# A feed-forward convolution whose third tap moves from VectorE to ScalarE and an adding DMA transfer

## The chip, the cores and the metric

The kernel runs on one core of a Trainium2 chip. The metric is the device time of one execution in microseconds (us). A profile of one execution gives the start and duration of each instruction on TensorE (PE, with its weight loads as PEld), VectorE (DVE), ScalarE (ACT), GpSimd (POOL) and the DMA queues that SyncE (SP) and GpSimd issue.

## What is computed

One layer of a hybrid decoder: a mixer (stick-breaking attention beside a gated convolution), then a feed-forward block with a causal convolution of three taps between its up-projection and its activation. The change lies in the feed-forward block. Its reference, for 1024 positions and 1024 channels, with 2 x 2816 columns of `w_up`:

```python
def causal_dwconv(u, w):              # y[t] = w[0] u[t-2] + w[1] u[t-1] + w[2] u[t]
    up = jnp.pad(u, ((0, 0), (kw - 1, 0), (0, 0)))
    y = up[:, 0:s, :] * w[0]
    for i in range(1, kw):
        y = y + up[:, i:i + s, :] * w[i]
    return y

h = rms_norm(x, norm_ffn_pre[l])
u = causal_dwconv(h @ w_up[l], conv_ffn_w[l])
a, g = jnp.split(u, 2, axis=-1)
f = (jax.nn.gelu(g, approximate=True) * a) @ w_down[l]
x = x + rms_norm(f, norm_ffn_post[l])
```

## The kernel before

Channels lie on the 128 partitions and positions along the free dimension, so the 2816 columns of a and of g are 22 tiles f of 128 channels, each a buffer of 128x1024 float32. Products are made with float16 pairs (a high half and a low half of each operand), three matmuls for one product, in block schemes that save one block product in eight: each tile f has seven products, `up_prod(f, 1..7)`, of twelve matmuls each. Their sums leave PSUM by ScalarE copies and VectorE additions into two buffers `ca` and `cg`. The bank `b` of a tile takes the products 1, 6, 7 and 4 in turn, so the eviction of one must be over before the next starts.

`up_done(f)` then runs `conv` for `ca` into `ua` and for `cg` into `ug`: ScalarE writes `u = w2 * c` (line 1527), VectorE adds the taps with lags 1 and 2 (line 1529, two instructions). ScalarE applies gelu to `ug` in place (line 1539), VectorE multiplies it into `ua` (line 1540), and ScalarE sums the squares (line 66) for the scale of the float16 halves.

The tiles are in six groups of 4, 4, 4, 4, 3 and 3. The sums of squares of a group are added over partitions by a one-column matmul `pr_f` on TensorE from VectorE's `rb_f`; its result `sp_f` scales the halves `fa`, `fy`, `fs` and `fx` (high half by ScalarE on line 824, low half by VectorE on line 826). For each of the first four groups a stage follows of seven products with `w_down`, each in four tiles of positions (`pq`, line 1656). ScalarE evicts `pq` to `st` (line 1660), and GpSimd's queue adds each `st` of 512 KB to a partial sum `acc` in memory (line 790; the first group writes plainly). One more pair of up-products, that of product 4 and `up_done` of the tile f in hand, stands inside each stage behind its first product. Weights are loaded by SyncE (`ws_u`, `ds`), their squares summed by ScalarE (`jk_u`), reduced through `rb_u` and `pr_u` like the above, and converted into `wh_u` and `wq`. `join` reads the partial sums back (`u`, `yacc`), and the last two groups are multiplied plainly into `pd` (lines 1726 and 1759), whose VectorE evictions add to `yacc`; the closing norm and the output follow.

The order on every engine is written by a planner, `Plan`: each step has an engine, a cost, the buffers that it reads and writes, and perhaps a due time; TensorE's main products keep the order of the program (`seq`), and the rest is placed by readiness and lateness, in a model that counts buffers, too. Large buffers (`ca`, `cg`, `ua`, `ug`, `st`, `ds`, the halves) share 16 slots of one pool, `slab`; a slot is taken again when its last reader is done. An engine runs its instructions in the order written, and so does each DMA queue issue.

Of the kernel before, what the change touches and what calls it, by code (L numbers as in the profile page):

```python
# [20 lines left out]
AF = mybir.ActivationFunctionType  # L21
ALU = mybir.AluOpType
# [3 lines left out]
T = 1024  # L26
# [4 lines left out]
NFF = FF // P  # L31
# [16 lines left out]
class Layer:  # L48
# [692 lines left out]
    def rest(self):  # L741
# [14 lines left out]
        C = dict(Asq=0.82, A=0.97, Ah=0.5, As=1.04, Ash=0.6, Aq=1.18, V=1.21, Vh=0.64, Vp=0.72)  # L756
        vec, act, pe = nc.vector, nc.scalar, nc.tensor

        DUE = {"conv": 20.0, "fin": 25.0, "ev": 3.0, "pass": 5.0, "hn": 14.0}
# [19 lines left out]
        def V(cost, fn, r, w, **kw):  # L779
            return pl.add("V", cost, fn, r, w, **kw)  # L780

        def A(cost, fn, r, w, **kw):
            return pl.add("A", cost, fn, r, w, **kw)
# [4 lines left out]
        def load(eng, b, dst, srcf, mb=1.45, r=(), w=None, ahead=None, **kw):  # L788
            e = nc.sync if eng == "SP" else nc.gpsimd
            j = pl.add(eng, 0.45 if eng == "SP" else 1.14, lambda: e.dma_start(dst(), srcf(), **kw), r,  # L790
                       [b] if w is None else w, ahead=AHEAD["load"] if ahead is None else ahead)
            j.load, j.lag = mb, pl.LAG[eng]
            return j
# [40 lines left out]
        AHEAD = dict(load=45.0, sq=40.0, up=32.0, quad=40.0, wq=60.0, wp=40.0, join=20.0, pr=3.0, cv=1.0, ca=1.0, mb=2.7)  # L834
        AHEAD.update(self.ahead_set)
        C = {k: v * AHEAD["ca" if k[0] == "A" else "cv"] for k, v in C.items()}
# [631 lines left out]
        def up_prod(f, i):  # L1468
# [16 lines left out]
            def vadd(o, oc, og, x, xr):  # L1485
                V(C["Vp"], lambda: vec.tensor_tensor(o.t[:, oc], b.t, x.t[:, xr[0]], ALU.add),
                  [b, (x, xr[1])], [(o, og)])
# [17 lines left out]
            else:  # L1505
# [13 lines left out]
                else:  # L1519
                    vadd(cg, lo, "l", cg, (lo, "l"))  # L1520

        def conv(f, u, c, idx, name):
            p = up[f]
            sm = Buf("sm", lambda: self.small(f"cw_{name}{f}"))
            V(0.25, lambda: vec.tensor_scalar(sm.t[:, 0:3], self.cfw[:, idx, :], p.sb.t["inv"], self.inv_h2, ALU.mult, ALU.mult),
              [p.sb], [sm])
            A(C["A"], lambda: act.activation(u.t, c.t, AF.Copy, scale=sm.t[:, 2:3]), [c, sm], [u])  # L1527
            for lag in (1, 2):
                V(C["V"], lambda lag=lag: vec.scalar_tensor_tensor(u.t[:, lag:], c.t[:, :T - lag], sm.t[:, 2 - lag:3 - lag],  # L1529
                                                                  u.t[:, lag:], ALU.mult, ALU.add), [c, sm], [u], due=DUE["conv"])  # L1530

        smb = [note() for _ in range(ng)]

        def up_done(f):
            p = up[f]
            g = max(g for g in range(ng) if ff0[g] <= f)
            conv(f, p.ua, p.ca, f, "a")
            conv(f, p.ug, p.cg, NFF + f, "g")
            A(C["A"], lambda: act.activation(p.ug.t, p.ug.t, AF.Gelu_apprx_tanh), [], [p.ug])
            V(C["V"], lambda: vec.tensor_tensor(p.ua.t, p.ug.t, p.ua.t, ALU.mult), [p.ug], [p.ua], due=DUE["fin"])  # L1540
            A(C["Aq"], lambda: self.sumsq(p.ua.t, smfs[g][:, f - ff0[g]:f - ff0[g] + 1], f"f{f}"), [p.ua], [smb[g]])
# [521 lines left out]
```

## Time and profile before

| | |
|---|---|
| median of three runs | 1243.44 us (1242.54 to 1244.03) |
| profiled execution | 1242.53 us, span of its instructions 1240.8 us |
| granted TensorE clock | 0.999 |
| DMA packets moved | 160.80 MB, mean 130 GB/s |

The page gives the busy time of each engine and its share of the span, then the groups of instructions by line. A group's row has the count behind an x, busy time and mean, and the idle time of its engine just ahead with what ended it. A row of the timeline has the start and duration in us, the engine, the line, what is written and read, and in brackets the idle time before with its releaser. A row of stretches has the busy time of each engine in it, TensorE's granted clock, the mean share of the 16 DMA engines and the GB/s that they moved.

The parts of the span: the mixer to about 640 us; the feed-forward tiles from there to 1171.6 us with the four stages of `pq` beginning at about 733, 842, 951 and 1060 us; then the plain products to 1234 us and the close.

### The profile page before, as it was taken

What the parts mean: (1) busy time and instruction counts of PE and PEld (TensorE: products, weight loads), DVE (VectorE), ACT (ScalarE), POOL (GpSimd) and SP (SyncE); (2) the same over time, 40 slices, a digit from 0 to 9 for tenths busy, and PEclk for the clock granted to TensorE, in tenths of its full rate; (3) what the DMA queues carried; (4) which work ended last, traced back from release to release, by engine and by line L of the source; (5) the groups of instructions that cost most, each with busy time, mean ns of one, the idle gap of its engine ahead of it and who ended that gap; (6) DMA issues with size and microseconds to landing.
All of it is one profiled execution on the core that took longest, in us unless ns stands there. A gap on an engine that the chain in (4) does not pass through costs nothing.

```text
span 1240.8 us, 16493 instructions
## 1 busy us (share of the span) xinstructions
PE 1227.5 (99%) x6041; PEld 556.4 (45%) x6041; DVE 1044.5 (84%) x1652; ACT 861.3 (69%) x1252; POOL 86.6 (7%) x113
## 2 busy tenths in 40 slices
PE   9999999999999999999999999999999999999997
PEld 4444444444444444444444444444444444444443
DVE  7888879856998998859899999799599779959876
ACT  7766666736779666646666679678778867878434
POOL 1100000000000000001100002002100300211003
PEclk9999999999999999999999999999999999999999
DMA  8755577660253122446953305316921961694608
GB/s 277 157 126 123 136 128 169 162 154 18 74 194 123 52 65 71 156 133 163 211 144 101 103 34 225 149 34 113 260 68 26 209 174 35 110 246 143 180 1 136
DMA packets 148931, 160.80 MB, mean 130 GB/s; under 512 B 114425, under 2 KB 114553, under 8 KB 148850
## 3 DMA queue, kind: packets, MB, share of 16 engines
q1 hardware_dynamic: 138480, 123.05, 35.9%
q0 software_dynamic: 10368, 36.70, 14.2%
q8 instruction: 47, 0.77, 0.3%
q14 instruction: 34, 0.28, 0.1%
q10 hardware_dynamic: 2, 0.00, 0.0%
HBM read 92.88 MB, written 37.75 MB: 105 GB/s over the span
## 4 chain that ended last, share of the span: by engine, by line
PE 91%; DVE 4%; DMA 1%; issue 1%; ACT 1%; POOL 1%; POOLq 0%; DVEq 0%; ACTq 0%
PE pq L1656 12%; PE pcc L459 3%; PE pq L459 3%; PE py L1283 3%; PE pk L459 3%; PE pywa L923 3%; PE pv L367 3%; PE pd L1726 2%; PE z L595 2%; PE o L595 2%; PE pd L1759 2%; DMA ws_u<-w_up_nt 1%; PE pga L459 1%; PE pg3b L1030 1%; PE pb0b L1030 1%
## 5 line engine op out<-in xcount | busy, mean ns | idle before, releaser
L1480 PEld LDWEIGHTS <-wh_u 128*128 128x128 f16 x1848 | 179.0, 98 | 216.4 <-issue 1.6
L1030 PEld LDWEIGHTS <-wh_g 128*128 128x128 f16 x588 | 57.1, 98 | 69.5 <-issue 1.0
L824 ACT ACTIVATE wh_u<-ws_u,sc_u 128x1024 f16<-128x1024 f32 (+1 forms) x66 | 66.3, 1007 | 29.5 <-DVE sc_u L809 7.5
L1283 PE MATMUL py<-wo,m 128*128 128x512 f16 x384 | 83.7, 379 | 0.0
L1660 ACT ACTIVATE st<-pq,sd 128x512 f32<-128x512 f32 x112 | 74.7, 693 | 9.4 <-PE pq L1656 6.6
L826 DVE SCALAR_TENSOR_TENSOR wh_u<-ws_u,sc_u,wh_u 128x1024 f16<-128x1024 f32 (+1 forms) x66 | 72.3, 1103 | 7.1 <-ACT wh_u L824 6.8
L790 POOL DMA_DIRECT2D acc<-st x56 | 43.7, 781 | 424.9 <-ACT st L1660 424.9
L624 DVE TENSOR_TENSOR_SCAN e<-e,mask 128x512 f32<-128x512 f32 (+3 forms) x64 | 48.7, 807 | 13.3 <-ACT e L617 13.3
L1529 DVE SCALAR_TENSOR_TENSOR ug<-cg,cw_g,ug 128x1023 f32<-128x1023 f32 (+1 forms) x44 | 56.2, 1278 | 2.2 <-ACT ug L1527 2.2
L1283 PEld LDWEIGHTS <-m 128*128 128x128 f16 x384 | 37.4, 98 | 44.9
L1529 DVE SCALAR_TENSOR_TENSOR ua<-ca,cw_a,ua 128x1023 f32<-128x1023 f32 (+1 forms) x44 | 56.2, 1277 | 1.3 <-ACT ua L1527 1.2
L617 ACT ACTIVATE e<-z,cz 128x1024 f32<-128x1024 f32 (+3 forms) x48 | 42.3, 895 | 20.4 <-PE z L595 14.9
L66 ACT ACTIVATE jk_u<-ws_u 128x1024 bf16<-128x1024 f32 x44 | 46.3, 1053 | 13.3 <-DMA ws_u<-w_up_nt 13.1
L638 ACT ACTIVATE w<-e 128x1024 f16<-128x1024 f32 (+3 forms) x48 | 38.8, 837 | 12.3 <-DMA wt<-w 7.5
L459 PE MATMUL pcc<-hT,wh_cc 128*128 128x512 f16 x192 | 44.5, 380 | 0.8 <-ACT u L575 0.8
L459 PE MATMUL pk<-hT,wh_k 128*128 128x512 f16 x192 | 43.1, 379 | 0.0
L459 PE MATMUL pq<-hT,wh_q 128*128 128x512 f16 x192 | 43.0, 379 | 0.0
L1656 PE MATMUL pq<-wq,fx 128*128 128x512 f16 x192 | 42.8, 379 | 0.0
L1656 PE MATMUL pq<-wq,fy 128*128 128x512 f16 x192 | 42.7, 379 | 0.0
L1656 PE MATMUL pq<-wq,fs 128*128 128x512 f16 x192 | 42.2, 379 | 0.0
L624 DVE TENSOR_TENSOR_SCAN e<-e,cr,mask 128x512 f32<-128x512 f32 x32 | 39.8, 1272 | 1.3 <-ACT e L617 1.1
L826 DVE SCALAR_TENSOR_TENSOR wh_u<-s_u,sc_u,wh_u 128x1024 f16<-128x1024 f32 x22 | 28.2, 1280 | 13.4 <-ACT wh_u L824 13.2
(846 smaller groups left out, 2777.8 us busy)
## 6 DMA issues: line engine op xcount, KB each, us to landing
acc<-st POOLq DMA_DIRECT2D x56, 512.0 KB, 6.0
ws_u<-w_up_nt SPq DMA_DIRECT2D x44, 512.0 KB, 3.9
ds<-w_down SPq DMA_DIRECT2D x18, 512.0 KB, 15.3
wt_g<-w_in_nt SPq DMA_DIRECT2D x14, 512.0 KB, 3.5
x<-x SPq DMA_DIRECT2D x8, 512.0 KB, 8.6
wr_wo<-w_out SPq DMA_DIRECT2D x8, 512.0 KB, 5.4
ws_wo<-w_out SPq DMA_DIRECT2D x8, 512.0 KB, 3.7
xr<-x SPq DMA_DIRECT2D x8, 512.0 KB, 4.3
```

Source lines behind the costliest of these rows:

```text
L66: self.nc.scalar.activation(self.junk(f"jk_{name}"), src, AF.Square, accum_out=acc)
L459: pe.matmul(ps.t, w.t[:, wi, ds(k * P, P)], hT[:, hi, k, ds(c * NH, NH)], start=k == 0 and p == 0, stop=k == KD - 1 and p == 2)
L595: pe.matmul(out, w, mv, skip_group_check=True, **kw)
L624: vec.tensor_tensor_scan(x, x, m[:, ::-1], ONE if diag else cr.t[:, h:h + 1], ALU.mult, ALU.max)
L824: A(C["As" if big else "Ash"], lambda: act.activation(dst.t[:, 0, dsl], src.t[:, ssl], AF.Copy, scale=sb.t["s"]), [(src, sreg), sb], [(dst ...
L826: V(C["V" if big else "Vh"], lambda: vec.scalar_tensor_tensor(dst.t[:, 1, dsl], src.t[:, ssl], sb.t["s"], dst.t[:, 0, dsl], ALU.mult, ALU. ...
L1030: pe.matmul(b.t, p.w[wt].t[:, wi, ds(wc * NH + k * P, P)], block(i, h, k), start=first and n == 0, stop=n == 3 * KH - 1, skip_group_check= ...
L1283: pe.matmul(b.t, m16[k].t[:, h_, ds(tt * P, P)], wo[k].t[:, w_, sl], start=k == 0 and p == 0, stop=k == 7 and p == 2)
L1480: pe.matmul(b.t, p.w[wt].t[:, wi, ds(wc * NH + k * P, P)], block(i, h, k), start=first and n == 0, stop=n == 3 * KH - 1, skip_group_check= ...
L1529: V(C["V"], lambda lag=lag: vec.scalar_tensor_tensor(u.t[:, lag:], c.t[:, :T - lag], sm.t[:, 2 - lag:3 - lag], u.t[:, lag:], ALU.mult, ALU ...
L1656: pe.matmul(b.t, fa[p].t[:, h, ds(fo * NH + tt * P, P)], wa[p].t[:, x, ds(wo * NH, NH)], start=first and n == 0, stop=n == 5, skip_group_c ...
L1660: A(C["Ah"], lambda tt=tt, b=b, st=st: act.activation(st.t[:, tt % 2, :], b.t, AF.Copy, scale=q.sd.t[:, 0:1]), [b, q.sd], [(st, str(tt % 2 ...
```

## The change

The tap with lag 2 is no longer a VectorE instruction. ScalarE scales `c` in place by w0, once the tap with lag 1 has read it, and a transfer issued by GpSimd adds `c[0:1022]` to `u[2:1024]`, both in the on-chip memory SBUF. `TAPS` names the tiles f for which this is done: all 22, for `ua` and `ug` each, so 44 VectorE instructions go, 44 ScalarE instructions and 44 transfers of 128 rows of 4088 bytes come.

```diff
+        TAPS = range(NFF)
+
         def conv(f, u, c, idx, name):
...
             A(C["A"], lambda: act.activation(u.t, c.t, AF.Copy, scale=sm.t[:, 2:3]), [c, sm], [u])
-            for lag in (1, 2):
-                V(C["V"], lambda lag=lag: vec.scalar_tensor_tensor(u.t[:, lag:], c.t[:, :T - lag], sm.t[:, 2 - lag:3 - lag],
-                                                                  u.t[:, lag:], ALU.mult, ALU.add), [c, sm], [u], due=DUE["conv"])
+            V(C["V"], lambda: vec.scalar_tensor_tensor(u.t[:, 1:], c.t[:, :T - 1], sm.t[:, 1:2], u.t[:, 1:], ALU.mult, ALU.add),
+              [c, sm], [u], due=DUE["conv"])
+            if idx % NFF in TAPS:
+                A(C["A"], lambda: act.activation(c.t, c.t, AF.Copy, scale=sm.t[:, 0:1]), [sm], [c], due=DUE["conv"])
+                load("G", None, lambda: u.t[:, 2:], lambda: c.t[:, :T - 2], r=[c], w=[u], mb=AHEAD["mb"], ahead=1e9,
+                     accum_op=ALU.add)
+            else:
+                V(C["V"], lambda: vec.scalar_tensor_tensor(u.t[:, 2:], c.t[:, :T - 2], sm.t[:, 0:1], u.t[:, 2:], ALU.mult, ALU.add),
+                  [c, sm], [u], due=DUE["conv"])
```

Since the steps have other engines and costs, the planner writes another order from the feed-forward part on. Three places show it. Lines behind the change are eight higher (L1547 is the gelu of L1539, L1668 the eviction of L1660, L1739 that of L1731; L1529 the first scaling of L1527, L1533 the new one).

ScalarE at the entry of the third stage of `pq`, before: `ug_8599` is the gelu of the tile ahead, `st_1_0` the stage's first evictions.

```order
L824 ACTIVATE wq_6_8650<-ds_8227,sp_dn_8372 128x1024
L1489 ACTIVATE cg_8574<-pu13c 128x512
L1539 ACTIVATE ug_8599<-ug_8599 128x1024
L66 ACTIVATE jk_u_0_8687,sm_u_8686<-ws_u_0_8643 128x1024
L824 ACTIVATE fx_0_8697<-ua_7628,sp_f_8549 128x1024
L1660 ACTIVATE st_1_0_8708<-pq_0_1_8689,sd_8602 128x512
L824 ACTIVATE fs_0_8710<-ua_7836,sp_f_8549 128x1024
```

The same place after the change.

```order
L1489 ACTIVATE ca_8641<-pu13b 128x512
L1533 ACTIVATE cg_8449<-cg_8449,cw_g_8202 128x1024
L824 ACTIVATE fa_8668<-ua_7661,sp_f_8612 128x512
L824 ACTIVATE fa_8668<-ua_8282,sp_f_8612 128x512
L1489 ACTIVATE cg_8591<-pu13c 128x512
L824 ACTIVATE fy_0_8693<-ua_7843,sp_f_8612 128x1024
L824 ACTIVATE fy_1_8695<-ua_8429,sp_f_8612 128x1024
L66 ACTIVATE jk_u_0_8713,sm_u_8712<-ws_u_0_8658 128x1024
L1547 ACTIVATE ug_8621<-ug_8621 128x1024
L1668 ACTIVATE st_1_0_8735<-pq_0_1_8717,sd_8671 128x512
```

The halves `fa` and `fy`, which stood ahead of the copy of pu13c, now stand on both sides of it, and the gelu, which reads what the transfer adds to, stands right ahead of the stage's first eviction.

GpSimd's queue at the same stage: before, it holds the partial sums alone.

```order
L790 DMA acc_0_5175<-st_1_0_8708 128x1024
L790 DMA acc_1_5176<-st_1_2_8732 128x1024
L790 DMA acc_0_5177<-st_2_0_8772 128x1024
L790 DMA acc_1_5178<-st_2_2_8798 128x1024
L790 DMA acc_0_5183<-st_5_0_8819 128x1024
```

After the change the convolutions' transfers stand among them.

```order
L790 DMA ua_8573<-ca_8496 128x1022
L790 DMA ug_8621<-cg_8449 128x1022
L790 DMA acc_0_5175<-st_1_0_8735 128x1024
L790 DMA acc_1_5176<-st_1_2_8762 128x1024
L790 DMA acc_0_5177<-st_2_0_8801 128x1024
L790 DMA acc_1_5178<-st_2_2_8824 128x1024
L790 DMA ug_8803<-cg_8591 128x1022
L790 DMA acc_0_5183<-st_5_0_8849 128x1024
L790 DMA ua_8833<-ca_8641 128x1022
```

Two come ahead of the stage's first partial sum, and two, of the tile that is finished inside the stage, between the partial sums.

VectorE in the plain products, at the scale of the last group's halves: `rb_f` goes to TensorE's `pr_f`, and `f_5_0` is the first low half. Before:

```order
L803 CAST rb_f_10692<-sp_f_10691 128x1
L1731 SCALAR_TENSOR_TENSOR yacc_10403<-pd_3_0_10668,sd_10430,yacc_10403 128x512
L1731 SCALAR_TENSOR_TENSOR yacc_10403<-pd_3_1_10681,sd_10430,yacc_10403 128x512
L1731 SCALAR_TENSOR_TENSOR yacc_10350<-pd_4_0_10696,sd_10430,yacc_10350 128x512
L807 TENSOR_SCALAR sp_f_10691<-pr_f_10707 128x1
```

After:

```order
L803 CAST rb_f_10748<-sp_f_10747 128x1
L1739 SCALAR_TENSOR_TENSOR yacc_10383<-pd_4_0_10736,sd_10411,yacc_10383 128x512
L1739 SCALAR_TENSOR_TENSOR yacc_10383<-pd_4_1_10751,sd_10411,yacc_10383 128x512
L1739 SCALAR_TENSOR_TENSOR yacc_10399<-pd_5_0_10762,sd_10411,yacc_10399 128x512
L807 TENSOR_SCALAR sp_f_10747<-pr_f_10775 128x1
```

The scale comes behind the eviction of `pd_5_0` and no longer of `pd_4_0`, so `pr_f` has moved two products of nine matmuls later.

## The prediction

> **What bounds the kernel now.** I read the busy table first, then the waits of TensorE, then the chain that ended last, then the feed-forward part by stretches.
>
> ```profile
> PE 1227.5 (99%) x6041; PEld 556.4 (45%) x6041; DVE 1044.5 (84%) x1652; ACT 861.3 (69%) x1252; POOL 86.6 (7%) x113
> PE 91%; DVE 4%; DMA 1%; issue 1%; ACT 1%; POOL 1%; POOLq 0%; DVEq 0%; ACTq 0%
> ...
> PE pu0c L1480 <- DMA hT<-n: 1.0, 1, 1.0
> ...
> 655.63 2.59 PE pu0b L1480 x12
> ...
> core 0: us, PE busy (x) PEld busy (x) DVE busy (x) ACT busy (x) POOL busy (x), PEclk, DMA share, GB/s
> 640.00:1172.00 532.00, 531.04 (x2486) 240.85 (x2484) 459.77 (x680) 406.02 (x564) 49.54 (x63) 1.00 0.49 130
> ```
>
> TensorE is busy 1227.5 of 1240.8 us and makes up 91% of the chain. The third row is the whole answer of the waits of TensorE from 630 us to the end: one wait of 1.0 us, before the feed-forward products proper. In 640 to 1172 us, where every instruction of the change lies but the last few, TensorE is busy 531.04 of 532.00 at granted clock 1.00, while VectorE has 72 us and ScalarE 126 us idle. Twelve matmuls of 512 columns take 2.59 us, 216 ns each, one behind the other. So work taken off VectorE buys nothing there directly; it can only keep a margin. The change can lengthen the time as soon as TensorE waits.
>
> **The change, part by part.** These rows price what goes and what comes.
>
> ```profile
> L1529 DVE SCALAR_TENSOR_TENSOR ug<-cg,cw_g,ug x44: 1271/1278/1285, 661.3 to 1178.3; 128x1023 f32<-128x1023 f32 x22, 128x1022 f32<-128x1022 f32 x22
> L1527 ACT ACTIVATE ug<-cg,cw_g x22: 1133/1142/1156, 659.9 to 1172.4; 128x1024 f32<-128x1024 f32 x22
> L1539 ACT ACTIVATE ug<-ug x22: 1044/1054/1061, 665.7 to 1179.9; 128x1024 f32<-128x1024 f32 x22
> L1540 DVE TENSOR_TENSOR ua<-ug,ua x22: 1211/1218/1226, 666.8 to 1182.2; 128x1024 f32<-128x1024 f32 x22
> ...
> q0 software_dynamic: 10368, 36.70, 14.2%
> ...
> out<-o POOLq DMA_DIRECT2D x7, 512.0 KB, 5.4
> u<-acc POOLq DMA_DIRECT2D x2, 512.0 KB, 10.4
> ...
> L790 POOL DMA_DIRECT2D acc<-st x14: 862/862/865, 955.2 to 992.1; - x14
> DMA to landing us min/median/max: 5.3/7.7/15.5
> ```
>
> Removed: 44 VectorE taps (the 22 of 128x1022 on ug in the first row, and 22 on ua) of 1.28 us, 56 us, none of it on the chain. Added to ScalarE: 44 in-place scalings of 128x1024, 1.14 us each as the row of the first scaling, 50 us; its 406 us of 532 become about 456, hidden as long as each lands in idle time. Added to GpSimd: 44 issues of 0.86 us, 38 us on a queue that is 7% busy. Added to the DMA engines: queue q0 took 14.2% of the span, 176 us of all 16 engines, for 36.70 MB, so 2.5 us per 512 KB; 44 transfers make 111 us, on engines whose mean share is about half.
>
> The latency is the unknown: no transfer before adds from SBUF into SBUF. The nearest rows are adding transfers of the same size. At the quiet end `out<-o` lands 5.4 us after issue; between the crowded partial-sum transfers of one stage `acc<-st` takes 5.3 to 15.5, and `u<-acc`, which adds into SBUF in the crowded join, 10.4. I take 5.4 where the queue is quiet and about 8 inside the stages, and keep 5.3 and 15.5 as ends. The Trainium skill has a fit for such a transfer ("DMA: Bandwidth & Descriptors", Anatomy of one DMA — SWDGE (gpsimd) path): about 2.0 us and the bytes by 436 GB/s, here an estimate of 3.2 us. By it every margin below grows by 2 us and the sum stays; the adding rows here are slower than that.
>
> So each conv gets a longer chain: 1.28 us of VectorE become 1.14 + 0.3 + 5.4, some 5.6 us more. Whether TensorE feels that is decided where its margin is smallest. The planner has moved its neighbours for it; three places matter.
>
> *First, the entry of the four-member stage* (third of four; the fourth has the same order).
>
> ```profile
> 865.38 1.25 ACT L1660 ACTIVATE st<-pq,sd 128x512 f32<-128x512 f32 x2
> ...
> 941.24 2.17 ACT L824 ACTIVATE fy<-ua,sp_f 128x1024 f16<-128x1024 f32 x2
> ...
> 943.34 2.75 PE L1480 MATMUL pu13c<-hB,wh_u 128*128 128x512 f16 x12
> ...
> 946.12 0.60 ACT L1489 ACTIVATE cg<-pu13c 128x512 f32<-128x512 f32 x1 [0.15 <-PE pu13c L1480]
> ...
> 947.57 1.05 ACT L66 ACTIVATE jk_u<-ws_u 128x1024 bf16<-128x1024 f32 x1
> ...
> 951.11 5.34 PE L1656 MATMUL pq<-wq,fa 128*128 128x512 f16 x24
> 952.60 0.69 ACT L1660 ACTIVATE st<-pq,sd 128x512 f32<-128x512 f32 x1 [0.99 <-PE pq L1656]
> ...
> 956.28 1.27 DVE L826 SCALAR_TENSOR_TENSOR fs<-ua,sp_f,fs 128x1024 f16<-128x1024 f32 x1
> ...
> 964.05 2.75 PE L1656 MATMUL pq<-wq,fs 128*128 128x512 f16 x12
> ...
> 946.00:952.00 6.00, 6.00 (x30) 2.69 (x29) 5.61 (x10) 3.73 (x5) 0.00 (x0) 1.00 0.00 1
> ```
>
> The fs halves are ready at 957.55 now and used at 964.05, a margin of 6.5 us. In the changed order `pr_f` stands two products later (behind the second pu13b product, so at 943.3 by these rows), and the gelu `ug<-ug` of the last conv stands on ScalarE ahead of the first eviction `st_1_0`, now waiting for the transfer. Its in-place scaling ends at about 945.2 (copy of ca 943.5 to 944.1, then 1.14), issue 945.5; the DMA engines are idle there (share 0.00), so it lands at 950.9, and the gelu (1.05) is done at 952.0, before the eviction's 952.6. From there to the end of fs_1 ScalarE has four evictions at 0.62 (1.25 for two), one sum of squares at about 1.1 with its read-out, and fx_0, fs_0 and fs_1 at 1.08 each (2.17 for two), together 6.8 us to 959.4; VectorE's low half, 1.27, ends at 960.7, a margin of 3.3 us. It is used up when the transfer takes more than 5.4 + 0.6 + 3.3, about 9.3 us. Cost: none.
>
> *Second, inside and at the end of a stage.*
>
> ```profile
> 946.10:992.80 46.70, 46.70 (x220) 21.22 (x219) 38.46 (x58) 39.76 (x59) 11.95 (x14) 1.00 0.78 157
> ...
> 988.32 1.06 ACT L66 ACTIVATE jk_u<-ws_u 128x1024 bf16<-128x1024 f32 x1 [2.08 <-DMA ws_u<-w_up_nt]
> 989.69 0.16 DVE L803 CAST rb_u<-sc_u 128x1 bf16<-128x1 f32 x1
> 992.60 0.17 PE L812 MATMUL pr_u<-rb_u,ones 128*128 128x1 bf16 x1
> 992.79 0.60 ACT L1489 ACTIVATE cg<-pu14b 128x512 f32<-128x512 f32 x1 [1.02 <-PE pr_u L812]
> 995.21 2.75 PE L1480 MATMUL pu14b<-hB,wh_u 128*128 128x512 f16 x12
> ```
>
> ScalarE is busy 39.76 of 46.70 us between the copies of pu13c and pu14b. Two scalings (2.3 us) come in, and the two fy conversions (2.1 us) move in from ahead: 44.2, so 2.5 us idle where now are 6.9. Of these 0.99 (first product) and 2.08 (weights) are forced, so the copy of pu14b comes about 0.6 us later; TensorE needs its bank at 995.21, 1.8 us behind the copy's end now. Cost: none, margin about 1.2 us. The stage's two transfers (5 us of DMA work) stand between the partial sums in GpSimd's queue; what is queued behind them, `acc` and with it the slots of `st`, comes up to 5 us later; the eviction st_7_0 needs st_5_0's slot some 8 us after its issue, just about the landing I take. `pr_u`, now 2.75 us behind `rb_u`, stands two products later, so a late weight load has 5 us more.
>
> *Third, the close.*
>
> ```profile
> 1172.44 1.15 ACT L1527 ACTIVATE ug<-cg,cw_g 128x1024 f32<-128x1024 f32 x1
> L790 POOL DMA_DIRECT2D yacc<-acc x4: 862/982/1333, 1143.7 to 1147.1; - x4
> ...
> 1184.78 0.16 DVE L803 CAST rb_f<-sp_f 128x1 bf16<-128x1 f32 x1
> ...
> 1189.06 0.17 PE L812 MATMUL pr_f<-rb_f,ones 128*128 128x1 bf16 x1
> 1189.93 0.15 DVE L807 TENSOR_SCALAR sp_f<-pr_f 128x1 int32<-128x1 int32 x1
> 1191.90 3.67 DVE L826 SCALAR_TENSOR_TENSOR f<-ua,sp_f,f 128x1024 f16<-128x1024 f32 x3
> 1198.80 27.36 PE L1759 MATMUL pd<-wdh,f 128*128 128x512 f16 x126
> ```
>
> On GpSimd's queue the last but one conv's transfers stand behind the join's `yacc`, issued by 1148.4 (1147.1 and 1.3), before that conv has its sums; even with 15.5 us from an issue near 1160 (my estimate) they land about when the last conv's second scaling ends. For the last conv: the scaling of ug ends 1173.6, tap 1174.9, second scaling 1176.1, two transfers land by 1176.4 + 5.4 + 2.5 = 1184.3, product and sum of squares 2.5, so `rb_f` at about 1187.4 for 1184.9. `pr_f` now stands 18 matmuls later, 1189.06 + 3.9 = 1192.9: margin 5.5. The three low halves then start behind the eviction of pd_5_1 at 1195.6 and end at 1199.3; the last is needed by the sixth matmul of the last group, 1198.80 + 5 x 0.216 = 1199.9. Margin 0.6, cost none. From there to the end nothing changes.
>
> **The sum.** No term reaches the chain; for a dozen margins that shrink to about 1 us I add 0.5 us. The profiled execution, 1242.53 us, becomes 1243.0; the median of the three runs is 0.9 above it: 1243.9.
>
> **The rivals.**
>
> *The transfer lands late (slower).* One mechanism: the gelu at a stage's entry holds ScalarE, which evicts for TensorE. It decides from a landing of 9.3 us. For it: `u<-acc` took 10.4, and the tail of `acc<-st` 15.5. Against: those waited in a crowded queue, and at 945 the engines are idle. At 12 us each of the last two stages loses 2.7, together 5.4: 1249; at 15.5, 12: 1256.
>
> *ScalarE overflows (slower).* If waits for slots or transfers add 3 us to a stage's ScalarE, 1.2 of them are covered, and 1.8 us reach TensorE in each of two stages, less in the others: 3 to 5 us, 1247 to 1249. For it: ScalarE has 2.5 us left there.
>
> *The crowded engines hold back the weights (slower).* Five more us of DMA work per stage, three crowded stages; if `jk_u` waits 7 instead of 2.08 us, the extra two products of `pr_u` are eaten and some 2 to 3 us per stage lost: 1250 to 1253. Against: weight loads are on the other queue, and q0 had a backlog there already.
>
> *VectorE was the pacer (faster).* If TensorE's matmuls are only stretched by late evictions, 56 us less VectorE could shorten the stream, at most to 1187. Against: VectorE is idle 72 of 532 us, and TensorE's one wait there is 1.0 us. The Trainium skill ("Perfetto Trace Analysis", Identifying the Most-Contended Engine) holds matmul busy time for a bad measure and asks for LDWEIGHTS busy, 45% here: by that rule TensorE would have room. The trace does not agree: 2484 loads of 97 ns (240.85 by 2484), one for each matmul of 216 ns, are 45% of a stream that has no gap.
>
> **Chances and range.** No change within 0.2% (2.5 us, about what the runs' own spread of 1.5 us allows to be told): 0.60. Late landing 0.16, ScalarE overflow 0.14, weights held back 0.05: slower 0.35. Faster 0.05. The range runs from 1241.8 (the fastest run less half the spread) to 1252.5, which leaves out the far end of the late landing, part of the held weights and the gain: about 0.15.
>
> **What will show it.** VectorE about 990 us busy, ScalarE about 910, GpSimd 44 issues more, q0 near 23% of the span. Right: TensorE's waits in the feed-forward stay under 2 us, and the gelu waits for a DMA only in ScalarE's own idle time. Wrong: rows of TensorE waiting for `st`, `fs`, `cg` or `rb` at the stages near 951, 992, 1060 and 1102 us, or the new transfers landing above 9 us.

## The result, and the profile after

The changed kernel takes 1248.81 us (median of 8 runs, 1246.62 to 1253.34), the kernel before 1242.9 (8 runs beside it, 1241.45 to 1244.03): ratio 1.0051, 95% interval 1.0041 to 1.006, so some 6 us slower. The forecast of 1243.9 was missed by 5 us; 1248.81 lies inside the range and where two of the slower rivals stood, but that is luck: most of the loss came at a place that none of the rivals named. The profiled execution of the changed kernel took 1248.08 us, span 1246.4, which is 5.6 us more than before; this is the growth that the rows below have to account for.

From its page: the busy table, the chain, GpSimd's queue, and the landings (size and median us from issue) of the new transfers.

```profile
PE 1228.0 (99%) x6041; PEld 556.5 (45%) x6041; DVE 996.4 (80%) x1608; ACT 902.5 (72%) x1296; POOL 125.7 (10%) x157
...
q0 software_dynamic: 16704, 59.73, 24.2%
...
PE 81%; issue 6%; DVE 5%; ACT 4%; DMA 3%; POOL 1%; SPq 0%; POOLq 0%; DVEq 0%; ACTq 0%
...
ua<-ca POOLq DMA_DIRECT2D x22, 511.0 KB, 5.2
ug<-cg POOLq DMA_DIRECT2D x22, 511.0 KB, 4.6
```

The work moved as the change says: VectorE 48 us less, ScalarE 41 more, GpSimd 44 instructions more. TensorE's busy time is the same, but its share of the chain fell from 91% to 81%: other engines and the DMA now stand in the chain. The waits of TensorE from 630 us to the end name the places (us in total, times, longest).

```profile
PE pu21b L1480 <- DVE cg L1486: 1.9, 1, 1.9
PE pu0c L1480 <- DMA hT<-n: 1.6, 2, 1.0
PE pu20c L1480 <- ACT cg L1489: 0.8, 1, 0.8
PE pu2c L1480 <- ACT ug L1511: 0.6, 1, 0.6
PE pq L1664 <- ACT st L1668: 0.2, 1, 0.2
```

Before, only the second line was there, with 1.0 us. I compared the start of each product with the same product before. It is 0.6 us later behind pu0c (both programs are the same up to there, and the kernel c_vec_add below, no slower than before, waits there for 1.7 us, too: this is not the change). Then 0.8 us more are lost at pu2c, 0.6 in the second stage of `pq`, 1.0 at pu20c and 2.1 at pu21b; 0.4 lies behind the last matmul. So 4.5 us of waits came with the change, and 3.1 of them at the join, where the partial sums are read back.

The join in the timeline of the changed kernel:

```profile
1141.00 0.87 POOL L790 DMA_DIRECT2D ua<-ca  x1 [11.93 <-ACT ca L1533]
...
1141.39 20.91 SPq L790 DMA_DIRECT2D yacc<-acc  x16
...
1149.60 1.15 ACT L824 ACTIVATE f<-ua,sp_f 128x1024 f16<-128x1024 f32 x1 [2.12 <-DMA ua<-ca]
...
1150.65 0.58 ACT L1489 ACTIVATE cg<-pu20c 128x512 f32<-128x512 f32 x1
...
1151.28 2.75 PE L1480 MATMUL pu20c<-hT,wh_u 128*128 128x512 f16 x12 [0.81 <-ACT cg L1489]
...
1169.02 0.69 DVE L1699 TENSOR_TENSOR yacc<-yacc,u 128x512 f32<-128x512 f32 x1 [0.95 <-DMA yacc<-acc]
...
1171.58 0.69 DVE L1699 TENSOR_TENSOR yacc<-yacc,u 128x512 f32<-128x512 f32 x1 [0.68 <-DMA yacc<-acc]
...
1173.39 0.68 DVE L1486 TENSOR_TENSOR cg<-pu21b,cg 128x512 f32<-128x512 f32 x1
...
1174.12 2.75 PE L1480 MATMUL pu21b<-hT,wh_u 128*128 128x512 f16 x12 [1.94 <-DVE cg L1486]
```

Tile 19's `ua` transfer, issued at 1141.0, meets the readings `yacc`. ScalarE's conversion `f` waits for its landing. `f` does not read tile 19, so what it waits for must be the slot of `ca`, which the transfer reads. The copy of pu20c stands behind `f` in ScalarE's order, and TensorE waits for that bank. Some 20 us later VectorE waits for the readings themselves, and the addition that frees pu21b's bank stands behind these. The same stretch of 32 us by its engines, before and then after:

```profile
1140.00:1172.00 32.00, 32.00 (x150) 14.51 (x149) 27.82 (x39) 20.21 (x28) 5.83 (x7) 1.00 0.87 240
```

```profile
1140.00:1172.00 32.00, 31.19 (x147) 14.04 (x146) 22.73 (x34) 24.71 (x32) 8.89 (x10) 1.00 1.05 260
```

VectorE and ScalarE are not full in either. The DMA engines (last but one number) nearly are: 0.87 of 32 us is 27.8 us of work before, which leaves 4 us on average, and the tiles 19 and 20 bring four transfers. Where tile 19's transfers fall nothing was left even before (the share adds up the packets' times, so it can pass 1):

```profile
1144.00:1152.00 8.00, 8.00 (x39) 3.64 (x38) 5.91 (x10) 5.22 (x10) 3.21 (x4) 1.00 1.02 279
1152.00:1160.00 8.00, 8.00 (x40) 3.64 (x39) 5.92 (x10) 5.23 (x6) 0.00 (x0) 1.00 1.09 257
```

A full stretch alone does not stop TensorE, though: it is busy throughout in these rows, and before the change the share was 1.04 from 856 to 896 us, too, with no wait. The SyncE readings land in a median of 15.9 us for 11.5 before.

The other two places, timeline of the changed kernel:

```profile
670.47 1.28 ACT L1547 ACT_TABLE_LOAD   x1
...
671.76 1.06 ACT L1547 ACTIVATE ug<-ug 128x1024 f32<-128x1024 f32 x1
...
677.03 0.58 ACT L1511 ACTIVATE ug<-pu2c 128x512 f32<-128x512 f32 x1
...
677.66 2.53 PE L1480 MATMUL pu2c<-hT,wh_u 128*128 128x512 f16 x11 [0.62 <-ACT ug L1511]
...
868.58 0.69 ACT L1668 ACTIVATE st<-pq,sd 128x512 f32<-128x512 f32 x1 [1.38 <-DMA ug<-cg]
...
874.08 4.04 PE L1664 MATMUL pq<-wq,fy 128*128 128x512 f16 x18 [0.16 <-ACT st L1668]
```

The first gelu and its table load stood at 664.42 before, in ScalarE's idle time; now, planned behind the transfer, they stand in a full stretch, and the copy of pu2c comes 0.6 us too late. In the second stage, `st` waits until a transfer that reads `cg` has landed, after 9.8 us; again it must be the slot.

### The profile page after: what moved, and what is told of

The parts are those of the page before. It is cut to its first block, busy times and chain, and to the rows that moved or that the text cites. A ratio compares the mean times of both kernels' runs of the same rounds, so it can differ in the third digit from the quotient of the medians.

```text
span 1246.4 us, 16601 instructions
## 1 busy us (share of the span) xinstructions
PE 1228.0 (99%) x6041; PEld 556.5 (45%) x6041; DVE 996.4 (80%) x1608; ACT 902.5 (72%) x1296; POOL 125.7 (10%) x157
## 3 DMA queue, kind: packets, MB, share of 16 engines
q0 software_dynamic: 16704, 59.73, 24.2%
## 4 chain that ended last, share of the span: by engine, by line
PE 81%; issue 6%; DVE 5%; ACT 4%; DMA 3%; POOL 1%; SPq 0%; POOLq 0%; DVEq 0%; ACTq 0%
PE pq L1664 7%; PE pcc L459 3%; PE pq L459 3%; PE py L1283 3%; PE pk L459 3%; PE pywa L923 3%; PE pv L367 3%; PE pd L1734 2%; PE z L595 2%; PE o L595 2%; PE pd L1767 2%; PE pga L459 1%; ACT st L1668 1%; PE pu21b L1480 1%; PE pg3b L1030 1%
## 5 line engine op out<-in xcount | busy, mean ns | idle before, releaser
L1668 ACT ACTIVATE st<-pq,sd 128x512 f32<-128x512 f32 x112 | 76.5, 719 | 4.8 <-PE pq L1664 3.2
L790 POOL DMA_DIRECT2D ua<-ca x22 | 19.8, 901 | 237.0 <-ACT ca L1533 181.7
```

Of the source, the lines that this page charges most:

```text
L1668: A(C["Ah"], lambda tt=tt, b=b, st=st: act.activation(st.t[:, tt % 2, :], b.t, AF.Copy, scale=q.sd.t[:, 0:1]), [b, q.sd], [(st, str(tt % 2 ...
```

## The experiments

Two theories at first. **J**: the loss is at the join, by the transfers. **S**: the 44 scalings fill ScalarE. All twelve are set against the kernel before on the same chip.

**a_no_join and b_join_only: the tiles next to the join, left out and alone.**

```diff
-        TAPS = range(NFF)
+        TAPS = [f for f in range(NFF) if f not in (18, 19, 20)]   # a; b: (18, 19, 20)
```

> The tiles 18, 19 and 20, whose transfers fall next to the join's reading of the partial sums, keep their lag-2 tap on VectorE; the other 19 tiles use ScalarE and the transfer as in the changed kernel. Theory J (the join): of the 5.6 us that the changed kernel's span is longer, 3.1 arise between 1141 and 1174 us, where the transfers of these tiles, the in-order queue of GpSimd and the 20 readings of partial sums meet; so this kernel is about 3 us faster than the changed one, some 2.5 to 3 us above the kernel before (ratio 1.002), with no wait of TensorE at pu20c or pu21b. Theory S (ScalarE): the loss is spread over all 44 in-place scalings; 38 of 44 remain, so 5 us above the kernel before (ratio 1.004).

> Only the tiles 18, 19 and 20 use the scaling and the transfer; all others keep the lag-2 tap on VectorE. Theory J: the join's loss is there alone, about 3 us above the kernel before (ratio 1.0025), in waits of TensorE near pu20c and pu21b. Theory S: 6 of 44 scalings remain, under 1 us, no difference that can be told (ratio 1.0007).

Measured: a 1.0032 (1.002 to 1.0045), b 1.0044 (1.0031 to 1.0058). Three of 22 tiles cost 5.5 us, far more than S allows; J is right on b's place, but had 3 us there. And a kept 4 us where J left 2.5 to 3, so the join is not all, or a new order has new losses (h_close). The profile of a, taken in the shortest of its five runs, shows only 1.8 us of new waits, 0.6 at pu2c and 1.2 at the close; the rest of the 4 us is open. In b, TensorE waits at pu20c for the same reason as above, only longer, and something comes on top (timeline of b, then its stretches):

```profile
1150.53 1.15 ACT L824 ACTIVATE f<-ua,sp_f 128x1024 f16<-128x1024 f32 x1 [4.50 <-DMA ua<-ca]
...
1151.58 0.58 ACT L1489 ACTIVATE cg<-pu20c 128x512 f32<-128x512 f32 x1
...
1152.21 4.14 PE L1480 MATMUL pu20c<-hT,wh_u 128*128 128x512 f16 x12 [3.33 <-ACT cg L1489]
1156.19 2.75 PE L1480 MATMUL pu21b<-hT,wh_u 128*128 128x512 f16 x12
```

```profile
1152.00:1156.30 4.30, 4.09 (x13) 1.57 (x13) 1.90 (x4) 2.34 (x5) 0.00 (x0) 0.64 1.07 248
```

After 3.33 us without work TensorE runs the next twelve matmuls in 4.14 us, not 2.75, at a granted clock of 0.64: 1.4 us more. J's other wait, at pu21b, is not there.

**c_vec_add: the scaling without the transfer.**

```diff
-                load("G", None, lambda: u.t[:, 2:], lambda: c.t[:, :T - 2], r=[c], w=[u], ..., accum_op=ALU.add)
+                V(1.22, lambda: vec.tensor_tensor(u.t[:, 2:], c.t[:, :T - 2], u.t[:, 2:], ALU.add), [c], [u], due=DUE["conv"])
```

> All 22 tiles keep the in-place scaling on ScalarE, but VectorE adds the scaled third tap (44 plain additions of 128x1022) in place of the transfer; GpSimd and the DMA engines are as before the change. Theory J, and any theory that puts the loss on the transfers (their landing, the buffers they hold, the traffic): time of the kernel before within 0.1 to 0.2%. Theory S: the loss of the changed kernel stays, 4 to 6 us (ratio 1.004 to 1.005).

Measured: 0.9997 (0.9988 to 1.0006). Its waits of TensorE from 630 us on:

```profile
PE pu0c L1480 <- DMA hT<-n: 1.7, 2, 1.0
```

44 scalings more on ScalarE (903.2 us busy) cost nothing. S falls; the loss is the transfers' (or the order that they bring).

**d_write: the transfer writes over instead of adding.**

```diff
-                     accum_op=ALU.add)
+                     )
```

> As the changed kernel, with the same buffers, order of issue and waits, but the transfer writes over u instead of adding to it, so the sum of the two nearer taps is lost. If adding is what makes the transfer dear on the DMA engines (it reads the target, too), the queue's share falls from 24.2% to nearer 19%, the landing in quiet places from 4.6-5.2 us to nearer 4, and theory J then expects half of the join's loss, about 1.5 us less than the changed kernel. If the price is the issue and the bytes alone, landing, share and time stay as in the changed kernel. Theory S: the same time as the changed kernel.

Measured: 1.0011 (1.0002 to 1.002), with the same order on each engine. From its page:

```profile
q0 software_dynamic: 13888, 59.73, 18.8%
...
ua<-ca POOLq DMA_DIRECT2D x22, 511.0 KB, 3.0
ug<-cg POOLq DMA_DIRECT2D x22, 511.0 KB, 2.9
```

The same bytes with 80 packets a transfer for 144 ((13888 - 10368) / 44, and the same of 16704). The DMA work of one is 1.3 us of all 16 engines for 2.85: 18.8% of 1242.5 us or 24.2% of 1246.4, less the 176 us of before, by 44. Four fifths of the loss go with the adding, where J had expected half of the join's.

**e_tile19, f_between, g_stage, h_close: the change in one place each.**

```diff
-        TAPS = range(NFF)
+        TAPS = (19,)     # f: [f for f in range(17) if f not in (5, 9, 13)]; g: (5, 9, 13, 17); h: (21,)
```

> Only tile 19 uses the scaling and the two transfers; its ones are issued at about 1141 and 1145 us, just as the readings of the partial sums begin, and in the kernel with tiles 18, 19 and 20 they landed 9.5 and 8.9 us after issue, while those of tile 18 took 4.7 and 5.6. Theory J19 (the late landing at the join keeps the slot of ca that ScalarE's conversions f need, and with it the copy of pu20c queued behind them): nearly all of the loss of the three tiles, 4 to 5.5 us above the kernel before (ratio 1.0035 to 1.0045), with a wait of TensorE of about 3 us at pu20c. Rival (the traffic of each of the three tiles counts alike, as DMA work in a full stretch): a third, 1.8 us (ratio 1.0015).

> Tiles 0 to 16 without 5, 9 and 13: 28 of the 44 transfers, all of them outside the four-member stages and ahead of the join; the other tiles keep the lag-2 tap on VectorE. Theory P (place decides: a transfer that meets no other traffic lands in about 5 us and costs nothing): only the wait of 0.6 us at pu2c, that the changed kernel has too, so 0.5 to 1 us above the kernel before (ratio 1.0004 to 1.001). Rival E (each transfer costs alike, the 4.0 us of the 38 transfers ahead of and behind the join): 28 of 38, 3 us (ratio 1.0024).

> Tiles 5, 9, 13 and 17 alone, whose eight transfers are issued inside the four-member stages, between the partial sums. Theory P: they land in 7 to 10 us and hold slots that the evictions st need, so the loss of the changed kernel ahead of the join that is not that of the close: 1.5 to 3 us above the kernel before (ratio 1.0012 to 1.0024), in waits of TensorE at pq for st. Rival E: 8 of 38 of 4.0 us, 0.8 us (ratio 1.0007).

> Tile 21 alone, whose two transfers stand in the plain products; the scale of the last halves f (pr_f) is 18 matmuls later than before. In the kernel without the tiles 18 to 20, TensorE waited 1.2 us there for the low halves f. Theory C (the close counts, since the margin of 0.6 us of the last low half is used up): 1 to 2 us above the kernel before (ratio 1.0008 to 1.0016). Rival (the margin holds): within 0.05% of the kernel before.

Measured: e 1.0009 (1.0001 to 1.0018), f 1.0013 (1.0004 to 1.0021), g 1.0004 (0.9995 to 1.0012), h 1.0017 (1.0009 to 1.0026). My J19 fell: tile 19 alone lost 1.1 us, which its rival's 1.8 us fits (the interval reaches to 1.0018). Its transfers landed as late as in b (9.5 and 8.6 us), but in this kernel's own order it was the gelu that waited for them (waits of ScalarE, then of TensorE):

```profile
ACT ug L1547 <- DMA ug<-cg: 3.7, 1, 3.7
```

```profile
PE pu21b L1480 <- DVE cg L1486: 0.2, 1, 0.2
```

So a late landing alone is not the price; what stands behind the waiting instruction is. In g, eight transfers inside the stages, landing in 6.7 to 8.4 us (medians), can't be told from nothing: theory P had too much there, and rival E's 0.8 us lies inside the interval. In f, rival E's 3 us is out; the loss is at pu2c, 1.7 us in its profile: 1.1 us of it the gelu's wait for the first `ug` transfer, at the place of the table load above. In h TensorE waits at the close:

```profile
PE pd L1767 <- DVE f L826: 1.2, 2, 0.6
```

There `pr_f` stood nine matmuls later than in the changed kernel, and a_no_join shows the same row; the changed kernel has no such wait. This loss, 1.7 thousandths in h, belongs to the orders of a and h. With b's 1.4 us of lowered clock (1.1 thousandths) it would account for the 2.5 by which a and b together exceed the whole; that is an estimate. The parts of a add up: f, g and h together give 3.4 thousandths, a 3.2.

**i_add_join, j_add_rest and l_write19: who adds, with nothing moved.** Since every other choice of tiles is a new order, these keep the changed kernel's and change only which transfers add.

```diff
+        ADDS = (18, 19, 20)     # j: all but 18, 19, 20; l: all but 19
...
+                kw = dict(accum_op=ALU.add) if idx % NFF in ADDS else {}
                 load("G", None, lambda: u.t[:, 2:], lambda: c.t[:, :T - 2], r=[c], w=[u], mb=AHEAD["mb"], ahead=1e9, **kw)
```

> The order of every engine is word for word that of the changed kernel, and all 44 transfers stand where they stood; but only those of tiles 18, 19 and 20 add, the other 38 write over (so their third tap's sum is lost). With all 44 writing the kernel was 1.4 us above the kernel before (ratio 1.0011). Theory T (adding doubles the DMA work of a transfer, and that matters where the engines are full already, at the join): 4.5 to 5.5 us above the kernel before (ratio 1.0036 to 1.0045), in TensorE's waits at pu20c and pu21b. Rival N (each adding transfer costs alike): 1.4 and 6 of 44 parts of 4.7 us, 2 us (ratio 1.0016).

> The order of the changed kernel again, and the complement: the 38 transfers of the other tiles add, the six of tiles 18, 19 and 20 write over (the third tap's sum is lost there). Theory T: the join's loss is gone, 1.5 to 2.5 us above the kernel before (ratio 1.0012 to 1.002), no wait of TensorE at pu20c and pu21b. Rival N: 1.4 and 38 of 44 parts of 4.7 us, 5.5 us (ratio 1.0044).

> The order of the changed kernel; all transfers add but the two of tile 19, which write over (its third tap's sum is lost). In the profile of the changed kernel both waits at the join come from the full engines between 1141 and 1172 us, into which tile 19 brings two transfers and tile 20 two. If tile 19's late landing (8.5 us, holding the slot that f needs) is the greater part: 2.5 to 3.5 us above the kernel before (ratio 1.002 to 1.003). If tile 20's transfers, issued at 1160 and 1167 us behind the readings, count as much, or the readings are late by themselves: 4.5 us or more (ratio 1.0036).

Measured: i 1.0031 (1.0022 to 1.0041), j 1.0003 (0.9994 to 1.0012), l 1.0011 (1.0003 to 1.0019). Rival N is out: 38 adding transfers cost nothing that can be told when the six write, six bring 3.1 of the 5.1 thousandths when the 38 write, and with only tile 19's two turned into writes 1.0051 becomes 1.0011. Theory T is right on the place, but each of the three came out below its forecast. And the parts do not add up: against d, where all 44 write, adding by the six brings 2.0 thousandths and adding by the 38 nothing, while both together bring 4.0 (each known to about one thousandth). Why the other 38 make the join dearer is open. Tile 19's `ua` transfer and the waits of TensorE in i, where both waits of the join are there:

```profile
L790 POOL DMA_DIRECT2D ua<-ca x1: 862/862/862, 1140.1 to 1140.1; - x1
...
DMA to landing us min/median/max: 8.6/8.6/8.6
```

```profile
PE pu21b L1480 <- DVE cg L1486: 1.5, 1, 1.5
PE pu0c L1480 <- DMA hT<-n: 1.0, 1, 1.0
PE pu20c L1480 <- ACT cg L1489: 0.9, 1, 0.9
PE pu2c L1480 <- ACT ug L1511: 0.6, 1, 0.6
```

The same of l, where neither is, and the stretch of 32 us:

```profile
L790 POOL DMA_DIRECT2D ua<-ca x1: 570/570/570, 1139.7 to 1139.7; - x1
...
DMA to landing us min/median/max: 6.0/6.0/6.0
```

```profile
PE pu0c L1480 <- DMA hT<-n: 1.3, 2, 1.0
PE pu2c L1480 <- ACT ug L1511: 0.6, 1, 0.6
...
1140.00:1172.00 32.00, 32.00 (x152) 14.54 (x150) 27.02 (x40) 24.64 (x31) 7.92 (x10) 1.00 1.03 280
```

So l's DMA engines are as full as the changed kernel's (1.03 for 1.05), with no wait of TensorE. What differs is when things land. The SyncE readings `yacc` land in a median of 15.8 us in i, 10.4 in l, 10.8 in j. They are a chain: SyncE issues the later ones only as earlier ones land. Its waits for that, in the changed kernel and then in l:

```profile
SPq L790 <- DMA yacc<-acc: 14.3, 8, 2.9
...
SPq L790 <- DMA yacc<-acc: 9.4, 9, 2.9
```

The last reading is issued at 1162.0 us in the changed kernel and at 1154.4 in l. In l tile 20's transfers add as before (its `ua` transfer takes 12.8 us in both), and GpSimd's own readings `u` stand behind tile 19's transfers as before, so neither makes the loss by itself.

**k_quiet: the change where it meets nothing.**

```diff
+        TAPS = [f for f in range(2, 17) if f not in (5, 9, 13)]
```

> The change on 12 tiles, 2 to 16 without 5, 9 and 13: 24 of 44 transfers, all between the stages, and neither the first tiles (where the gelu with its table load stands late in ScalarE's order) nor the join nor the close; the other tiles keep the lag-2 tap on VectorE. Theory P (place decides): the time of the kernel before, ratio 0.9995 to 1.0006, and no wait of TensorE behind 650 us. Rival (the 1.6 us of the 28 transfers between the stages are spread over them): 1.4 us above (ratio 1.0011). VectorE loses 24 x 1.28, 31 us; if that were worth anything, the time would fall below the kernel before.

Measured: 0.9996 (0.9988 to 1.0005). Stretch 640 to 1172 us:

```profile
640.00:1172.00 532.00, 531.45 (x2488) 241.07 (x2487) 434.12 (x654) 429.60 (x588) 70.54 (x87) 1.00 0.62 154
```

24 transfers cost nothing that can be told, and 26 us less of VectorE in this stretch (434.12 for 459.77) are worth nothing. No version tried is faster than the kernel before.

## Why the prediction was right or wrong

**What bounds.** Right. TensorE is the bound; VectorE's freed time bought nothing (k_quiet), so the rival of VectorE as the pacer is out.

**The prices.** Scaling (1.14), issue (0.87 us in the rows above) and busy times as told: VectorE 996 for 990, ScalarE 902 for 910, q0 24.2% for 23%. A transfer took 2.85 us of DMA work for 2.5. The landing, medians of 4.6 and 5.2 us for 5.4 in quiet places, was right, too. The Trainium skill's fit, 3.2 us, agrees with the writing transfer (2.9 to 3.0) and not with the adding one; the Trainium skill ("Collectives: The Full Stack", The bandwidth ceiling) has the reason for another program: an add in the DMA path needs two source reads for each write, there half the rate of a copy. The packets here, 144 for 80, and the work, 2.2 times, agree with that roughly; the case has no closer look at it.

**The entry of the stages.** Right: no wait of TensorE there; the transfers issued at 941 and 947 us landed in 5.2 and 4.5 us.

**Inside the stages.** The size was right: ScalarE was busy 44.09 of 47.0 us between the two copies, for the 44.2 of 46.7 forecast. A slot did come late, but that of `cg`, in the second stage: 0.6 us where I had none.

**The close.** For tiles 20 and 21 right: tile 20's `ua` transfer, issued at 1160.4, took 12.8 us of the 15.5 allowed, and the last low half ended 0.4 us before TensorE needed it, for a margin of 0.6 forecast. But the step looked only at these two. The transfers of tile 19 are issued as the readings of the join begin, and I weighed that stretch for what GpSimd's queue delays, not for the DMA work: 27.8 us in 32 before and four transfers of 2.5 give 37.8. This is the step that failed: tile 19 had no term, and in its place stand a landing of 8.5 us that holds a slot, and readings that land 4.4 us later in the median. It cost 3.1 of the 4.5 us. The DMA work, to be had from one row of the trace before, would have said that landings come late; that TensorE pays needs the second step as well, what is queued behind them, since l has 1.03 in that stretch and no wait.

**The sum.** The 0.5 us for a dozen margins stood for what measured 4.5 in waits; no change, given a chance of 0.60, did not come, and slower had 0.35. At the first tile I had no step at all: the gelu planned later, with the table load that the planner's order does not hide, made 0.8. By the prediction's own signs, too, it failed: TensorE's waits passed 2 us. But the other sign, landings above 9 us, misled: those of 10.4 and 12.8 us cost nothing visible, and the one of 8.5 did.

**The rivals.** The mechanism of "the transfer lands late" was right (a landing holds ScalarE, and an eviction that TensorE needs stands behind it), at another place, through a slot and not the gelu, and from 8.5 us. "ScalarE overflows": c_vec_add shows that the 44 scalings alone cost nothing; of the waits for slots that the rival adds to them, only the 0.6 us of the second stage came. "The crowded engines" were right in that traffic delays loads, but those of the join, not the weights.

What stays open: why the changed kernel's runs spread by 7 us (before: 3). The clock has a part in it: the mean granted clock is 0.996 in the longest of them, 1253.34 us, and 0.999 in the profiled one. The profile of j was taken in the longest of its runs, 1246.56 us for a median of 1243.97, and shows one way, at the wait at pu0c, which the kernel before has, too (timeline of j, then its stretch):

```profile
648.74 3.84 PE L1480 MATMUL pu0c<-hT,wh_u 128*128 128x512 f16 x11 [1.01 <-DMA hT<-n]
652.37 3.18 PE L1480 MATMUL pu0b<-hB,wh_u 128*128 128x512 f16 x12
...
650.00:655.00 5.00, 5.00 (x18) 1.86 (x16) 4.76 (x5) 3.69 (x4) 0.00 (x0) 0.68 0.31 82
```

In d, with the same order and nearly the same waits there, these two rows take 2.53 and 2.75 us at a clock of 1.00: j lost 1.7 us. No long run of the changed kernel itself was profiled.

## What to carry to other kernels

Before work is moved to a transfer, add its DMA work to every stretch where the engines are already near full, one by one: there it lands late, and so do the others. Here turning the adding of two of 44 transfers into writing took away four of the five thousandths. An adding transfer had the DMA work of about two writes; price it so. Then look at what is queued behind the instruction that waits for the landing, since a late landing costs only that; it includes instructions which merely reuse the buffer that the transfer reads.

## What was not expected of the hardware

Adding more than doubles the DMA work of a transfer: 2.85 for 1.3 us of the 16 engines, 144 for 80 packets, a median landing of 4.6 to 5.2 for 2.9 to 3.0 us, and a GpSimd issue of 0.87 for 0.54 to 0.57 us.

A wait of TensorE of 3.33 us was followed by twelve matmuls at a granted clock of 0.64, 4.14 for 2.75 us; one of 1.94 us, in the changed kernel, was not (2.75). The Trainium skill ("TensorE: Matmul & The Clock Gate", Part 1: The HAM clock gate) says that the clock is halved after an idle window of about 3.4 us and gets back after as long a busy one; these two rows fit that. The row of j does not fit as simply: there two waits of 0.83 and 1.01 us, with a matmul between them, were enough for a granted clock of 0.68 in the next 5 us, and in d two of 0.76 and 0.94 us were not.
